# Grouped-query attention on one core: the schedule table laid over 16 pairs of heads in place of 8, with 11 of 64 score tiles on VectorE

## The chip, the cores and the metric

The kernel runs on one NeuronCore of a Trainium2 chip, in one launch. The metric is device time in microseconds (us). TensorE (PE in the profile) multiplies matrices, and its weight loads have a row of their own (PEld); VectorE is DVE, ScalarE is ACT, GpSimd is POOL, and SyncE (SP) issues DMAs, as GpSimd does too. PSUM is the memory that TensorE writes to, SBUF the one that the other data lies in.

## The reference

```python
batch, seq, n_heads, n_kv_heads, dim = 8, 512, 32, 8, 64
scores = np.einsum('bhqd,bhkd->bhqk', Q, K_expanded) * scale      # scale = 1/8
weights = np.exp(scores - np.max(scores, axis=-1, keepdims=True))
weights = weights / (np.sum(weights, axis=-1, keepdims=True) + 1e-10)
output = np.einsum('bhqk,bhkd->bhqd', weights, V_expanded)
```

Four query heads share one K head and one V head (`np.repeat` on the head axis). Q, K and V are fp32 in HBM, the output is fp32.

## The kernel before

**Units and pairs.** The work is cut into 32 units: one batch and two neighbouring K heads (`gp`), with their eight query heads. A unit has 4 pairs of query heads, so there are 128 pairs. A pair has 4 score tiles, one for each 128 keys (`kc`): two matmuls put the scores of both heads, 128 keys by 512 queries each, into one PSUM tile of 128x1024 (`scores`, L235). There are 512 such tiles.

**The exponential on ScalarE.** For most tiles one ACTIVATE reads the PSUM tile and writes `pt` (`exp_act`, L253). These tiles lie in `s_ps`, of which there are two buffers: the scores of tile k can't begin before ScalarE has read tile k-2.

**The exponential on VectorE and GpSimd.** For the others (`DVE_KCS`) it is made of integer operations, in a chain of five instructions: `u`, scale and round from PSUM to 16-bit integers (`exp_bits`, L264, VectorE); `f`, the low ten bits (`exp_low`, L269, VectorE); `g`, a linear step (`slope`, L274, GpSimd); `w`, the product g*f (`bend`, L281, GpSimd); and the sum u+w, which is written as the bits of `pt` (`exp_join`, L285, VectorE). 5 of the 32 tiles of a period go this way.

**The second matmul.** For each pair 32 matmuls multiply `pt` with V; V carries a column of ones, so that each result has its row sum beside it (`pv`, L295). VectorE takes the reciprocal of the sums (`inverse`, L314) and multiplies (`norm`, L324). When a unit is complete, one DMA of 1 MB stores it; in the very last unit each pair has a store of its own, 256 KB (`norm`, `store`).

**PSUM regions.** Beside the two `s_ps` buffers there are two regions of the same size, `d_ps` (letter a in the table) and `pv` (letter b). Each holds one thing at a time: a VectorE score tile, the sums of a pair, or the turned Q of a half unit (`transposes`, L400, eight matmuls with the identity, then a VectorE copy, L194). The next user waits until VectorE has read the one before.

**Order.** Everything is issued in an order written out by hand, the table `STEPS`, which is walked once for each period of 8 pairs (two units, half a batch); `FINISH` replaces it in the last of the 16 periods (L530). A token is a letter and a number: `S` score tile for ScalarE, `A` its ACTIVATE, `V7.1-3` matmuls of pair 7, chunks 1 and 2 of 8 (4 matmuls each; the chunks 6 and 7 hold the keys whose exponential VectorE makes, where it makes one), `R` reciprocal, `N` normalisation, `T` and `C` turning Q and its copy, `K` and `H` a check of V and its reduction, `D` a score tile for VectorE, and `U F G W P` its chain (`g`, `w` in lower case: on VectorE instead). `Q` issues loads, `B` collects checks of the sums, `E` the end. `@1` means that the token belongs to the period before, `@-1` to the one after. An engine works in the order in which its own tokens stand; between engines semaphores decide. In what follows, step k is the stretch from `S`k to `S`k+1.

**Loads.** Q, K and V are loaded by GpSimd DMAs that convert to bf16 (L128 to L148); K is turned by DMA transposes on SP, followed by two copies between partitions (`dma_k`, L176). In a period, `Q0` loads K or V of the next batch, in turn, and `Q1` half a batch of Q two periods ahead (`loads`, L388). In the first period the start-up has its own loads, transposes on TensorE (`EARLY`, L213) and idle matmuls (`spin`, L487) in place of the missing tokens of a period before. In that period the tiles of the first two pairs all go to ScalarE (`on_dve`, L220).

Of the kernel before, what the change touches and what calls it, by code (L numbers as in the profile page):

```python
# [34 lines left out]
VV_HI = 1.0e30  # L35


DVE_KCS = ((3,), (3,), (), (3,), (), (3,), (3,), ())
STEPS = (
# [9 lines left out]
).split()  # L49
FINISH = (  # L50
# [31 lines left out]
def fast_path(ctx, tc, Q, K, V, out, flag):  # L82
# [32 lines left out]
    off = const_pool.tile([128, PPAIR * 2 * SC], U32, name="off")  # L115
# [94 lines left out]
    def early_k(gp, g, lo=0):  # L210
        return lambda bank: first_k(gp, g, bank, lo)

    EARLY = {0: [early_k(0, 0, SC // 2)], 1: [early_q(0, 1)], 2: [early_k(0, 1)],  # L213
             4: [early_q(1, 0)], 5: [early_k(1, 0)], 6: [early_k(1, 1)]}

    every = [(p, kc) for p in range(PPAIR) for kc in range(SC)]
    ON_DVE = [(p, kc) for p, kc in every if kc in DVE_KCS[p]]
    ON_ACT = [(p, kc) for p, kc in every if kc not in DVE_KCS[p]]

    def on_dve(n, k):  # L220
        return n * PPAIR + ON_DVE[k][0] >= NPAIR
# [49 lines left out]
            out=st["f"], in_=st["u"], scalar=1023, op=ALU.bitwise_and  # L271
        )

    def slope(engine, f, g):  # L274
        engine.tensor_scalar(  # L275
            out=g, in0=f, scalar1=-EXP_F1,
            scalar2=EXP_K * 2.0 ** (24 * (engine is nc.gpsimd)),
            op0=ALU.add, op1=ALU.mult,
        )

# [27 lines left out]
                    stop=(n == SC - 1 and qc == SC - 1),  # L308
                )

    RCOLS = PPAIR * 2 * SC
    right = const_pool.tile([128, RCOLS + 1], BF16, name="right")

    def inverse(p):  # L314
        n, k = divmod(p, PPAIR)
        if n not in invs:
            invs[n] = inv_pool.tile([128, PPAIR, 2, SC], FP32, name="inv")
        s = 0 if p % UPAIR < NPAIR else D
        nc.vector.reciprocal(out=invs[n][:, k], in_=sums[p][:, :, :, s:s + 1])  # L319
        done["inv", n] = done.get(("inv", n), 0) + 1  # L320
        if n == NPER - 1 and done["inv", n] == PPAIR:
            last_check()

    def norm(p):  # L324
        u, b, gp, g, i = place(p)
        if u not in osb:
            osb[u] = osb_pool.tile([128, SC, 2 * HPG, D], FP32, name="o_sb")
        h = 2 * (p % UPAIR)
        o = 1 - g
        nc.vector.tensor_tensor(  # L330
            out=osb[u][:, :, h:h + 2, :].rearrange("p qc m d -> p m qc d"),
            in0=sums.pop(p)[:, :, :, o:o + D],
            in1=invs[p // PPAIR][:, p % PPAIR, :, :, None].to_broadcast((128, 2, SC, D)),
            op=ALU.mult,
        )
# [6 lines left out]
    def bulk_check(n):  # L342
        nc.vector.scalar_tensor_tensor(  # L343
            out=off, in0=invs[n].rearrange("p s m qc -> p (s m qc)").bitcast(U32),
            scalar=INV_BITS, in1=off, op0=ALU.bitwise_xor, op1=ALU.bitwise_or,
        )
# [71 lines left out]
    def step(tok, n):  # L418
        what, k = tok[0], int(tok[1:].split(".")[0].rstrip("ab"))
        q, kc = ON_DVE[k] if what in "DUFGWPgwsa" else (0, 0)  # L420
        if what == "S":
# [4 lines left out]
                    copy()  # L426
            if k == 9 and n == 0:
                dma_k(0, TURNED)
            if k == 2 and n % 2 == 1 and n // 2 + 1 < B:
                dma_k(n // 2 + 1)  # L430
        elif what == "A":
            q, kc = ON_ACT[k]
            p = n * PPAIR + q
# [8 lines left out]
        elif what in "VRN":  # L442
            p = n * PPAIR + k
            if what == "V":
                lo, hi = tok[3:].rstrip("abs").split("-")
                pv(p, int(lo), int(hi), tok)
            else:
                (inverse if what == "R" else norm)(p)
        elif what in "TKCH":
            j = n * PPAIR // NPAIR + k  # L450
            if j < 2:
                pass
            elif what == "T":
                transposes(j, region(tok))
            elif what == "K":
                check_values(j)
            else:
                read(j if what == "C" else (j, "v"))
        elif what == "Q":
            loads(n, k)  # L460
        elif what == "B":
            if n < NPER - 1:
                bulk_check(n)
        elif what == "E":
            (early_check, verdict)[k]()
        elif what in "sa":
            (fill if what == "s" else exp_act)(n * PPAIR + q, kc)
        elif on_dve(n, k):
            p = n * PPAIR + q
            if what == "D":  # L470
                exp_fill(p, kc, region(tok))
                return
            st = chain.get((p, kc))
            if what == "U":
                exp_bits(st)
            elif what == "F":
                exp_low(st)
            elif what in "Gg":
                slope(nc.gpsimd if what == "G" else nc.vector, st["f"], st["g"])
# [48 lines left out]
    nc.vector.tensor_copy(out=kn[0][:, mid:hi, 0:2, :], in_=k_start[1][:, mid:hi, :, :])  # L528

    for period in range(-2, NPER):  # L530
        for entry in STEPS if period < NPER - 1 else FINISH:
            tok, _, late = entry.partition("@")
            n = period - int(late or 0)
            if 0 <= n < NPER:
                step(tok, n)
            elif period == 0 and n < 0 and tok[0] == "V":
                lo, hi = tok[3:].rstrip("abs").split("-")
                spin(int(hi) - int(lo), S // 4)
# [117 lines left out]
```

## Time and profile before

| | us |
|---|---|
| median of 3 runs (411.78 to 411.85) | 411.80 |
| the profiled execution | 411.91 |
| its span, first to last instruction | 410.1 |
| ScalarE busy in the span | 399.9 |
| TensorE busy (weight loads beside it: 242.2) | 377.7 |
| VectorE busy | 334.1 |
| GpSimd busy | 276.6 |

The 1.81 us between the span and the execution's time lie around the span. "Busy" is the union of the records of an engine; a matmul's record lasts longer than the time until the next can begin. In the rows of groups the columns are: line, engine, operation, written tile, read tiles, shape, count | busy us, mean ns of one | idle us before it and who ended it. In timelines: start us, duration us, engine, line, operation. In windows: from and to, length, then busy us and count for PE, PEld, DVE, ACT and POOL, granted TensorE clock, DMA share, GB/s.

### The profile page before, as it was taken

How to read it: one execution, taken by the hardware profiler on the slowest of the kernel's cores; microseconds unless marked ns; L12 is line 12 of the kernel's file. 1: busy time of each engine (PE TensorE's matmuls, PEld its weight loads, DVE VectorE, ACT ScalarE, POOL GpSimd, SP SyncE). 2: the span in 40 equal slices, each digit the busy share in tenths (PEclk: the TensorE clock that was granted, in tenths of full speed). 3: DMA queues.
4: the chain of work that ended last, by engine and by line, in shares of the span. 5: the costliest groups of instructions: out<-in, count | busy, mean ns of one | idle time of the engine just before them, and what ended most of it. 6: DMA issues, size and time to landing. Idle time of an engine off the chain costs nothing.

```text
span 410.1 us, 13319 instructions
## 1 busy us (share of the span) xinstructions
PE 377.7 (92%) x5824; PEld 242.2 (59%) x5824; DVE 334.1 (81%) x618; ACT 399.9 (98%) x437; POOL 276.6 (67%) x208
## 2 busy tenths in 40 slices
PE   7989999899998989989899998999989899998994
PEld 3556656565665656656565665656656566565663
DVE  2587888978889788797978889788798878889895
ACT  5999999999999999999999999999999999999994
POOL 9157776677666667676676776667776677765760
PEclk9999999999999999999999999999999999999999
DMA  9999876798659797479865888849788697762206
GB/s 149 196 195 153 192 154 178 181 172 175 159 149 187 119 247 160 140 180 250 158 143 117 193 221 155 206 106 172 195 156 202 160 172 167 157 173 104 78 29 209
DMA packets 65406, 67.74 MB, mean 165 GB/s; under 512 B 35264, under 2 KB 39872, under 8 KB 65344
## 3 DMA queue, kind: packets, MB, share of 16 engines
q0 software_dynamic: 28128, 24.91, 41.5%
q1 hardware_dynamic: 37216, 41.95, 33.7%
q8 instruction: 46, 0.75, 0.7%
q14 instruction: 16, 0.13, 0.1%
HBM read 50.33 MB, written 33.55 MB: 205 GB/s over the span
## 4 chain that ended last, share of the span: by engine, by line
ACT 77%; PE 20%; issue 1%; DVE 1%; ACTq 0%
ACT pt L254 77%; PE s_ps L240 9%; PE pv L303 6%; PE d_ps L303 4%; PE pv L492 1%; PE d_ps L191 0%; DVE qt L194 0%; ACTq L254 0%; DVE o_sb L330 0%; PE s_ps L191 0%; PE d_ps L170 0%; PE d_ps L202 0%; DVE warm L517 0%; DVE kt_first L172 0%; DVE off L343 0%
## 5 line engine op out<-in xcount | busy, mean ns | idle before, releaser
L254 ACT ACTIVATE pt<-s_ps 128x1024 f16<-128x1024 f32 x434 | 398.0, 1292 | 2.2 <-PE s_ps L240 2.2
L303 PEld LDWEIGHTS <-pt 128*128 128x128 f16 x4096 | 142.3, 98 | 64.9 <-issue 55.9
L240 PE MATMUL s_ps<-qt,kt 64*128 64x512 bf16 x810 | 158.7, 383 | 23.2 <-ACT pt L254 19.7
L283 POOL TENSOR_TENSOR w<-g,f 128x1024 bf16<-128x1024 bf16 x77 | 163.9, 2128 | 6.4
L275 POOL TENSOR_SCALAR g<-f 128x1024 bf16<-128x1024 int16 x77 | 80.8, 1049 | 113.2 <-DVE f L270 113.2
L303 PE MATMUL pv<-v,pt 128*128 128x65 bf16 x2560 | 113.9, 195 | 0.4 <-ACT pt L254 0.4
L240 PEld LDWEIGHTS <-kt 64*128 64x128 bf16 x960 | 57.5, 93 | 65.0 <-issue 34.5
L265 DVE TENSOR_SCALAR u<-d_ps 128x1024 int16<-128x1024 f32 x47 | 57.4, 1221 | 19.9 <-PE d_ps L240 19.9
L303 PE MATMUL d_ps<-v,pt 128*128 128x65 bf16 x1536 | 66.3, 194 | 0.0
L330 DVE TENSOR_TENSOR o_sb<-pv,inv 128x512 f32<-128x512 f32 x80 | 55.3, 691 | 2.7
L287 DVE TENSOR_TENSOR pt<-u,w 128x1024 uint16<-128x1024 int16 x78 | 53.4, 685 | 2.2 <-POOL w L283 0.8
L191 PEld LDWEIGHTS <-q_nat 128*128 128x128 bf16 x512 | 29.1, 98 | 15.1 <-issue 11.1
L265 DVE TENSOR_SCALAR u<-pv 128x1024 int16<-128x1024 f32 x31 | 37.7, 1216 | 0.0
L194 DVE COPY qt<-d_ps 128x1024 bf16<-128x1024 bf16 (+1 forms) x48 | 32.6, 680 | 3.7 <-PE d_ps L191 3.7
L330 DVE TENSOR_TENSOR o_sb<-d_ps,inv 128x512 f32<-128x512 f32 x48 | 33.2, 691 | 1.6
L270 DVE TENSOR_SCALAR f<-u 128x1024 int16<-128x1024 int16 x78 | 33.5, 429 | 0.1
L191 PE MATMUL d_ps<-ident,q_nat 128*128 128x128 bf16 x380 | 29.5, 220 | 0.1
L319 DVE RECIPROCAL inv<-pv 128x8 f32<-128x8 f32 x80 | 16.5, 206 | 10.5 <-PE pv L303 7.5
L319 DVE RECIPROCAL inv<-d_ps 128x8 f32<-128x8 f32 x48 | 9.9, 207 | 14.8 <-PE d_ps L303 14.3
L240 PE MATMUL d_ps<-qt,kt 64*128 64x512 bf16 x88 | 17.1, 375 | 0.0
L203 DVE TENSOR_REDUCE okv<-d_ps 128x1 f32<-128x128 f32 x31 | 8.9, 288 | 9.4 <-PE d_ps L202 9.3
L148 POOL DMA_DIRECT2D q_nat<-in_Q_dram x18 | 14.7, 815 | 0.0
(48 smaller groups left out, 112.8 us busy)
## 6 DMA issues: line engine op xcount, KB each, us to landing
out_dram<-o_sb SPq DMA_DIRECT2D x31, 1024.0 KB, 5.1
q_nat<-in_Q_dram POOLq DMA_DIRECT2D x15, 1024.0 KB, 8.9
k_nat<-in_K_dram POOLq DMA_DIRECT2D x7, 512.0 KB, 5.2
kt<-kt SPq DMA_DIRECT2D x14, 256.0 KB, 4.6
v<-in_V_dram POOLq DMA_DIRECT2D x7, 512.0 KB, 7.4
out_dram<-o_sb SPq DMA_DIRECT2D x4, 256.0 KB, 3.1
q_nat<-in_Q_dram POOLq DMA_DIRECT2D x1, 512.0 KB, 8.0
v<-in_V_dram POOLq DMA_DIRECT2D x4, 128.0 KB, 8.6
```

Of the source, the lines that this page charges most:

```text
L191: nc.tensor.transpose(ps[:, i, sc, :], qn[u // 2][:, sc, h:h + 2, :], ident)
L194: return lambda: nc.vector.tensor_copy(out=qt[u][:, g, lo:hi, :], in_=ps[:, lo:hi, :, :].rearrange("p i sc c -> p i (sc c)"))
L240: nc.tensor.matmul(ps[:, m, :], keys[64 * m:64 * m + 64, g if early else g ^ m, kc * 128:(kc + 1) * 128], qt[u][64 * m:64 * m + 64, g, i, ...
L254: nc.scalar.activation(out=pt_of(p)[:, kc, :, :], in_=filled.pop((p, kc)), func=EXP, scale=scale)
L265: nc.vector.tensor_scalar(out=st["u"], in0=st["ps"], scalar1=A_U, scalar2=B_U, op0=ALU.mult, op1=ALU.add)
L270: nc.vector.tensor_single_scalar(out=st["f"], in_=st["u"], scalar=1023, op=ALU.bitwise_and)
L275: engine.tensor_scalar(out=g, in0=f, scalar1=-EXP_F1, scalar2=EXP_K * 2.0 ** (24 * (engine is nc.gpsimd)), op0=ALU.add, op1=ALU.mult,)
L283: engine.tensor_tensor(out=w, in0=g, in1=f, op=ALU.mult)
L287: nc.vector.tensor_tensor(out=pt_of(p)[:, kc, :, :].bitcast(U16), in0=st["u"], in1=st["w"], op=ALU.add)
L303: nc.tensor.matmul(sums[p][:, m, qc, :], pt_of(p)[:, kc, m, qc * 128:(qc + 1) * 128], vt[b % 2][:, kc, gp, g * (D + 1):(g + 1) * (D + 1)], ...
L319: nc.vector.reciprocal(out=invs[n][:, k], in_=sums[p][:, :, :, s:s + 1])
L330: nc.vector.tensor_tensor(out=osb[u][:, :, h:h + 2, :].rearrange("p qc m d -> p m qc d"), in0=sums.pop(p)[:, :, :, o:o + D], in1=invs[p // ...
```

## The change

The table is laid over 16 pairs (four units, a whole batch) in place of 8, so there are 8 periods in place of 16. Of the 64 tiles of a period 11 go to VectorE, where two periods before had 10. In two of the eleven chains the product `w` runs on VectorE (`w2`, `w8`); nine stay on GpSimd. A period issues one K load, two Q loads (1 MB each) and one V load, at `Q0` to `Q3`. The first period has a table of its own, `FIRST`, and the last a new `FINISH`. In the first period the early transposes `EARLY` 4, 5 and 6 move one step ahead, and the idle matmuls have 64 columns in place of 128. The DMA transposes of K are issued at `S31` of each period in place of `S2` of each second one. The checks of the sums stay in groups of 8 pairs (`CPAIR`); `inv` has six buffers in place of three.

```diff
-DVE_KCS = ((3,), (3,), (), (3,), (), (3,), (3,), ())
+DVE_KCS = ((3,), (3,), (), (3,), (3,), (), (3,), (3,), (), (3,), (3,), (), (3,), (3,), (3,), ())
 STEPS = (
...
+    "A0 P10@1 V15.5-6@1 V13.0-1b@1 S1 F0 V15.6-7@1 Q0 A1 V15.7-8@1 V13.1-2@1 G0 V13.2-3@1 "
+    "R15@1 V13.3-4@1 N15@1 S2 A2 V13.4-8@1 W0 S3 R13@1 D2a A3 N13@1 S4 U2 V14.0-1b@1 A4 "
...
+    "A38 V9.2-4 S39 V9.4-5 P7 A39 V9.5-8 S40 F8 T7a R9 A40 B0@2 N9 G8 K7 S41 C7 A41 V10.0-3b "
+    "Q2 w8 S42 V10.3-4 A42 V10.4-6 H7 V10.6-7 P8 S43 A43 V10.7-8 F9 S44 R10 G9 D10a N10 A44 "
+    "U10 S45 V11.0-1b W9 V11.1-2 A45 V11.2-8 S46 R11 A46 N11 S47 V12.0-4a A47 P9 T0b@-1 F10 "
+    "S48 A48 C0@-1 V12.4-6 G10 V12.6-8 S49 R12 D1b@-1 A49 N12 S50 W10 U1@-1 T1a@-1 A50 K1@-1 "
+    "S51 A51 C1@-1 D0b@-1 S52 H1@-1 Q3 U0@-1 V15.0-1a A52 V15.1-4 S0@-1 V15.4-5 "
+).split()
+FIRST = (
...
+    "V14.2-4@1 P0 A5 V14.4-8@1 F1 S6 R14@1 A6 T2a G1 N14@1 S7 C2 D2a U2 Q0 A7 V0.0-3b W1 S8 "
+    "D3a A8 V0.3-4 U3 V0.4-5 S9 V0.5-6 A9 V0.6-8 S10 R0 P1 V2.0-2a A10 V2.2-4 F2 S11 N0 "
...
 FINISH = (
...
+    "V11.7-8 P9 V13.2-3 A49 S51 P10 V13.3-8 A50 R11 S52 R13 N13 A51 V15.0-2s E0 V15.2-4 N11 "
+    "V15.4-6 A52 V15.6-8 B0@2 V14.0-2a R15 V14.2-6 N15 V14.6-8 R14 N14 E1 "
...
     EARLY = {0: [early_k(0, 0, SC // 2)], 1: [early_q(0, 1)], 2: [early_k(0, 1)],
-             4: [early_q(1, 0)], 5: [early_k(1, 0)], 6: [early_k(1, 1)]}
+             3: [early_q(1, 0)], 4: [early_k(1, 0)], 5: [early_k(1, 1)]}
...
     def loads(n, k):
-        b, odd = divmod(n, 2)
-        if k == 0 and b + 1 < B:
-            (load_v if odd else load_k)(b + 1)
-        if k == 1 and n + 2 < NPER:
-            load_q(n + 2)
+        if n + 1 < B:
+            (lambda: load_k(n + 1), lambda: load_q(2 * n + 2),
+             lambda: load_v(n + 1), lambda: load_q(2 * n + 3))[k]()
...
-            if k == 2 and n % 2 == 1 and n // 2 + 1 < B:
-                dma_k(n // 2 + 1)
+            if k == 31 and n + 1 < B:
+                dma_k(n + 1)
...
     for period in range(-2, NPER):
-        for entry in STEPS if period < NPER - 1 else FINISH:
+        for entry in FIRST if period == 0 else STEPS if period < NPER - 1 else FINISH:
...
-                spin(int(hi) - int(lo), S // 4)
+                spin(int(hi) - int(lo), S // 8)
```

For comparison, the table of before has around its steps 6 to 10, and `FINISH` at its end:

```python
"V6.2-4@1 S6 P0 V6.4-6@1 A6 V6.6-7@1 F1 V6.7-8@1 S7 R6@1 G1 T2a N6@1 A7 S8 C2 V0.0-1b W1 "
"V0.1-2 A8 V0.2-3 S9 D2a V0.3-4 A9 U2 V0.4-5 S10 V0.5-7 A10 V0.7-8 B0@2 S11 P1 V1.0-2a "
...
"R6 V7.2-4 N6 V7.4-6 B0@2 A26 V7.6-8 R7 N7 E1 "
```

More of the change, by code (lines that the diff above doesn't have):

```diff
@@ L94, in fast_path @@
     TURNED = 2
+    CPAIR = PPAIR // 2
     scale = 1.0 / math.sqrt(D)
@@ L106, in fast_path @@
     osb_pool = ctx.enter_context(tc.tile_pool(name="osb", bufs=3))
-    inv_pool = ctx.enter_context(tc.tile_pool(name="inv", bufs=3))
+    inv_pool = ctx.enter_context(tc.tile_pool(name="inv", bufs=6))
     PS = bass.MemoryType.PSUM
@@ L114, in fast_path @@
     ident = const_pool.tile([128, 128], BF16, name="ident")
-    off = const_pool.tile([128, PPAIR * 2 * SC], U32, name="off")
+    off = const_pool.tile([128, CPAIR * 2 * SC], U32, name="off")
     okv = const_pool.tile([128, NU + 1], FP32, name="okv")
@@ L218, in fast_path @@
     ON_ACT = [(p, kc) for p, kc in every if kc not in DVE_KCS[p]]
+    BENT_BY_DVE = {int(t[1:].partition("@")[0]) for t in STEPS if t[0] == "w"}
     def on_dve(n, k):
@@ L272, in exp_low, with slope @@
         )
-    def slope(engine, f, g):
+    def slope(engine, f, g, small):
         engine.tensor_scalar(
-            out=g, in0=f, scalar1=-EXP_F1,
-            scalar2=EXP_K * 2.0 ** (24 * (engine is nc.gpsimd)),
+            out=g, in0=f, scalar1=-EXP_F1, scalar2=EXP_K * 2.0 ** (24 * small),
             op0=ALU.add, op1=ALU.mult,
@@ L309, in pv @@
                 )
-    RCOLS = PPAIR * 2 * SC
+    RCOLS = CPAIR * 2 * SC
     right = const_pool.tile([128, RCOLS + 1], BF16, name="right")
     def inverse(p):
-        n, k = divmod(p, PPAIR)
+        n, k = divmod(p, CPAIR)
         if n not in invs:
-            invs[n] = inv_pool.tile([128, PPAIR, 2, SC], FP32, name="inv")
+            invs[n] = inv_pool.tile([128, CPAIR, 2, SC], FP32, name="inv")
         s = 0 if p % UPAIR < NPAIR else D
@@ L320, in inverse @@
         done["inv", n] = done.get(("inv", n), 0) + 1
-        if n == NPER - 1 and done["inv", n] == PPAIR:
+        if n == 2 * NPER - 1 and done["inv", n] == CPAIR:
             last_check()
@@ L332, in norm @@
             in0=sums.pop(p)[:, :, :, o:o + D],
-            in1=invs[p // PPAIR][:, p % PPAIR, :, :, None].to_broadcast((128, 2, SC, D)),
+            in1=invs[p // CPAIR][:, p % CPAIR, :, :, None].to_broadcast((128, 2, SC, D)),
             op=ALU.mult,
@@ L342, in bulk_check @@
     def bulk_check(n):
+        done["checks"] = done.get("checks", 0) + 1
         nc.vector.scalar_tensor_tensor(
@@ L355, in last_check @@
     def last_check():
-        bulk_check(NPER - 1)
+        bulk_check(2 * NPER - 1)
+        assert done["checks"] == 2 * NPER
         nc.vector.tensor_single_scalar(
@@ L380, in probe @@
         nc.gpsimd.memset(f, 512)
-        slope(nc.gpsimd, f, g)
+        slope(nc.gpsimd, f, g, True)
         bend(nc.gpsimd, f, g, w)
@@ L444, in step @@
             if what == "V":
-                lo, hi = tok[3:].rstrip("abs").split("-")
+                lo, hi = tok.split(".")[1].rstrip("abs").split("-")
                 pv(p, int(lo), int(hi), tok)
@@ L461, in step @@
         elif what == "B":
-            if n < NPER - 1:
-                bulk_check(n)
+            if 2 * n + k < 2 * NPER - 1:
+                bulk_check(2 * n + k)
         elif what == "E":
@@ L478, in step @@
             elif what in "Gg":
-                slope(nc.gpsimd if what == "G" else nc.vector, st["f"], st["g"])
+                slope(nc.gpsimd if what == "G" else nc.vector, st["f"], st["g"],
+                      what == "G" and k not in BENT_BY_DVE)
             elif what in "Ww":
@@ L536, in fast_path @@
             elif period == 0 and n < 0 and tok[0] == "V":
[L537 to L538 removed]
+                lo, hi = tok.split(".")[1].rstrip("abs").split("-")
+                spin(int(hi) - int(lo), S // 8)
 def general_path(tc, Q, K, V, out):
```

58 rows, old and new, of tables (FINISH, FIRST, STEPS) are left out of this document.

## The prediction

> **What bounds the kernel now.** I read the chain of work that ended last first, then the groups, then the windows, one to a period.
>
> ```profile
> ACT 77%; PE 20%; issue 1%; DVE 1%; ACTq 0%
> L254 ACT ACTIVATE pt<-s_ps 128x1024 f16<-128x1024 f32 x434 | 398.0, 1292 | 2.2 <-PE s_ps L240 2.2
> ```
> ```profile
> 211.75:236.49 24.74, 23.13 (x364) 14.89 (x363) 20.80 (x39) 24.74 (x28) 17.12 (x12) 1.00 0.73 165
> 236.49:261.24 24.75, 23.12 (x364) 14.91 (x364) 20.81 (x39) 24.75 (x28) 17.75 (x12) 1.00 0.83 177
> ```
> ```profile
> L254 ACT ACTIVATE pt<-s_ps x434: 1018/1313/1349, 6.6 to 403.4; 128x1024 f16<-128x1024 f32 x145
> ```
>
> ScalarE is busy for all of each period (24.75 of 24.75 us, 27 tiles): one tile in 24.75/27 = 0.917 us. Its 434 tiles need 398 of the span's 410.1 us, and it was idle for 2.2 us, before its first tile. So the time is start + tiles x 0.917 + end, as long as every score tile is there when ScalarE wants it. How much later may one be? An ACTIVATE takes 1018 ns where it is quickest and 1313 in the median. I read the difference, 0.30 us, as time for which its record stands behind the one before: a score tile up to about 0.30 us late costs nothing, and what is beyond that ScalarE loses.
>
> **What goes: eight tiles.** Before, 16 x 27 tiles + 2 of the first pairs = 434. After, 8 x 53 + 2 = 426, as the built order of ScalarE shows too. The gain is 8 x 0.917 = **7.33 us**. The rest asks what the others make of a period of 53 x 0.917 = 48.6 us in place of two of 24.75 (49.5).
>
> **Engine sums for a period.** TensorE: the same matmuls (a tile moves from S to D); 2 x 23.13 = 46.3 of 48.6. VectorE:
>
> ```profile
> 248.75 0.21 DVE L319 RECIPROCAL inv<-pv 128x8 f32<-128x8 f32 x1
> 248.99 0.69 DVE L330 TENSOR_TENSOR o_sb<-pv,inv 128x512 f32<-128x512 f32 x1
> 249.60 1.22 DVE L265 TENSOR_SCALAR u<-d_ps 128x1024 int16<-128x1024 f32 x1
> 250.78 0.69 DVE L194 COPY qt<-pv 128x1024 bf16<-128x1024 bf16 x1
> 251.39 0.68 DVE L287 TENSOR_TENSOR pt<-u,w 128x1024 uint16<-128x1024 int16 x1
> 251.99 0.42 DVE L270 TENSOR_SCALAR f<-u 128x1024 int16<-128x1024 int16 x1
> 252.33 1.22 DVE L265 TENSOR_SCALAR u<-pv 128x1024 int16<-128x1024 f32 x1
> ```
> ```profile
> L283 DVE TENSOR_TENSOR w<-g,f 128x1024 bf16<-128x1024 bf16 x1 | 0.7, 682 | 0.0
> ```
>
> From start to start: R 0.24, N 0.61, U 1.18, C 0.61, P 0.60, F 0.34. A product on VectorE has a record as long as P's, so 0.60. One more chain is 2.12, two products are 1.20: 2 x 20.81 + 3.32 = 44.9 of 48.6, 92% against 84%. It still fits, but no longer with much room.
>
> The chain itself goes round: F, then GpSimd's g and w, then P, then the next F.
>
> ```profile
> 246.78 0.42 DVE L270 TENSOR_SCALAR f<-u 128x1024 int16<-128x1024 int16 x1
> ```
> ```profile
> 247.30 1.03 POOL L275 TENSOR_SCALAR g<-f 128x1024 bf16<-128x1024 int16 x1 [1.06 <-DVE f L270]
> 248.41 2.13 POOL L283 TENSOR_TENSOR w<-g,f 128x1024 bf16<-128x1024 bf16 x1
> ```
>
> F to the end of w is 3.76 us, P adds 0.60: 4.36 a round, and with the product on VectorE 0.52 + 1.03 + 0.05 + 0.60 + 0.60 = 2.80. Nine and two: 44.8 of 48.6, where ten took 43.6 of 49.5. That fits too, so on sums ScalarE stays the bound. What is lost must come from single places where a score tile is late.
>
> **Late tiles in every period.** TensorE works in order, so a step longer than 0.917 makes the next S late. The longest block of the trace:
>
> ```profile
> 398.30 0.39 PE L240 MATMUL s_ps<-qt,kt 64*128 64x512 bf16 x2
> 398.63 0.78 PE L303 MATMUL d_ps<-v,pt 128*128 128x65 bf16 x20
> 399.33 0.39 PE L240 MATMUL s_ps<-qt,kt 64*128 64x512 bf16 x2
> ```
> ```profile
> 403.20 1.04 PEld L303 LDWEIGHTS <-pt 128*128 128x128 f16 x32 [0.23 <-DVE right L351]
> ```
>
> 20 matmuls of a pair make a step of 1.03 us; 32 weight loads take 1.04, so 0.03 each. Step 45 holds all 32 matmuls of pair 11: 1.03 + 12 x 0.03 = 1.39, and S46 comes 0.47 late, 0.17 beyond the allowance. Step 47 (16 of pair 12, then T0) makes S48 about as late, but behind a loss that S46 has already cost. I followed the other steps with the intervals above, VectorE's waits included: S51 comes out at most 0.28 late (T1 waits for N12), S0 0.22, the others less. The term is 0.17 in each of the 7 periods that use this order: **+1.2 us**, from 0 (allowance 0.5) to 2.5 (S51 over it as well).
>
> **A hole in the first period.** In `FIRST`, step 7 puts `D2a` straight behind T2 in the same region: T2, its copy C2, D2, U2, D3 follow one another. In the other periods D2 stands at step 3. What such a row costs, the start of before shows:
>
> ```profile
> 14.25 0.39 PE L240 MATMUL s_ps<-qt,kt_first 64*128 64x512 bf16 x2
> 14.57 0.62 PE L191 MATMUL d_ps<-ident,q_nat 128*128 128x128 bf16 x8
> 15.23 0.69 DVE L194 COPY qt<-d_ps 128x1024 bf16<-128x1024 bf16 x1 [0.78 <-PE d_ps L191]
> ...
> 16.27 0.39 PE L240 MATMUL d_ps<-qt,kt_first 64*128 64x512 bf16 x2
> 16.59 0.42 PE L303 MATMUL pv<-v,pt 128*128 128x65 bf16 x8
> 16.70 1.23 DVE L265 TENSOR_SCALAR u<-d_ps 128x1024 int16<-128x1024 f32 x1 [0.78 <-PE d_ps L240]
> 16.97 0.39 PE L240 MATMUL s_ps<-qt,kt_first 64*128 64x512 bf16 x2
> ```
>
> From S6 at 0: T2 at 0.32, its copy ends 15.92 - 14.57 = 1.35 later (1.67), D2 at 1.72, U2 ends 0.43 + 1.23 later (3.38), D3 at 3.43. Behind D3 stand two chunks, and S9 follows 16.97 - 16.27 = 0.70 after D3: 4.13. It is due at 3 x 0.917 = 2.75; 1.38 late less 0.30 is **+1.1 us**, once (S8 is late by less on the way). Below: 0, if something ahead runs early; above: 1.4, without the allowance.
>
> **The end.** Before, ScalarE ended at 397.88 + 6.79 = 404.67, and 5.43 us followed.
>
> ```profile
> 397.88 6.79 ACT pt L254 x8
> ```
> ```profile
> 400.00:402.00 2.00, 2.00 (x45) 1.39 (x41) 1.97 (x5) 2.00 (x4) 0.00 (x0) 1.00 0.98 359
> 402.00:404.00 2.00, 1.95 (x44) 1.47 (x43) 1.36 (x6) 2.00 (x3) 0.00 (x0) 1.00 0.98 316
> ```
>
> After, behind the last A there stand not 8 matmuls but 40, since pair 14 comes wholly behind it: 32 x 0.03 = 0.96 later until the last R. Unit 30's store of 1 MB also moves: it waited for N3 at step 21 of 27, and now for N11 in the last step, about 0.5 us behind ScalarE's end. With the small stores about 1.8 MB then go out; at 340 GB/s, as in the windows, that is 5.4 us, about 1 us longer than the calculation hides. I take **+1.4 us**, from 0.9 (stores hidden) to 2.4 (nothing of them hidden).
>
> Costed at nothing: the loads. Q has 23 steps (21 us) from issue to first use, V 19 (17 us), against these landings (V is as large as K); if one took nearly twice as long it would still be there.
>
> ```profile
> q_nat<-in_Q_dram POOLq DMA_DIRECT2D x15, 1024.0 KB, 8.9
> k_nat<-in_K_dram POOLq DMA_DIRECT2D x7, 512.0 KB, 5.2
> ```
>
> SP issues the turning of K behind the store of the unit before, and TensorE first reads it at step 49. The early transposes and idle matmuls lie under the first ScalarE tiles.
>
> **Sum.** 410.1 - 7.33 + 1.2 + 1.1 + 1.4 = 406.5 of span; with the 1.81 around it 408.3; the profiled execution was 0.11 above the median, so **408.1 us** against 411.80.
>
> **The rivals.**
>
> *Nothing is lost inside.* If the allowance is wider than I read it and the first period's hole closes, 7.33 less 0.9 of end remains: 405.4. For it: two periods of before run without any loss at 93% of TensorE. Against: no step there was as long as 1.39.
>
> *VectorE becomes the bound (slower).* From step 40 to the next period's step 0 the order has for VectorE 3 F, 4 R, 4 N, 3 C, one product, 3 P, 3 U: 1.02 + 0.96 + 2.44 + 1.83 + 0.60 + 1.80 + 3.54 = 12.2 us, and three short checks, in 14 steps of 12.8 us. D0, D1, T0 and T1 of the next period wait for it, and behind them S. Twenty-four instructions that are each 0.03 us slower, or one wait of 0.7 that I overlooked, cost 0.6 in each of 7 periods, 4.2 us: from there the change loses. With 1.0 us it is 408.1 + 6.6 = 414.7. Against: these intervals repeat to 0.01 us from period to period.
>
> *VectorE and GpSimd hold each other up.*
>
> ```profile
> L270 DVE TENSOR_SCALAR f<-u x78: 415/420/1026, 18.0 to 397.0; 128x1024 int16<-128x1024 int16 x78
> ```
>
> One F took 1026 ns: it began while GpSimd was still in a product. A meeting of this kind costs 0.61 us, one in each period's full stretch 7 x 0.6 = 4.2 us: 412.2, no change. Against: in the table F of a chain stands directly behind P of the one before, P waits for GpSimd's w, and the next g waits for F, so GpSimd is between products when P and F run. [...]
>
> *An early load comes late.* In `FIRST` the K load of the next batch stands ahead of any product on GpSimd, directly behind the probe.
>
> ```profile
> 10.07 0.20 POOL L283 TENSOR_TENSOR probe_w<-probe_g,probe_f 128x2 bf16<-128x2 bf16 x1
> ...
> 21.66 0.62 POOL L131 DMA_DIRECT2D k_nat<-in_K_dram  x1
> ```
>
> So it starts some 11 us earlier than before, while the start-up's loads are still in flight. If the turned K of batch 0 came 2 us late for its first use (step 26), 408.1 + 2 = 410. Against: that use stands three steps later than before, since pair 8 has no tile on VectorE now.
>
> **Chances.** Forecast (406.8 to 409.8) 0.58; nothing lost 0.18; VectorE bound 0.13; holding up 0.06; late load 0.05. The range, 405.4 to 411.0, holds the first two and the last, 0.81; its ends are the bounds of the terms. A measurement here can tell 0.2%, 0.8 us, from no change: faster 0.58 + 0.18 + 0.05 = 0.81, same 0.06, slower 0.13.
>
> **What would show it.** 426 ACTIVATEs; ScalarE idle about 1.1 us between 14 and 18 us and about 0.17 before one tile in each 48.7 us; TensorE's waits there on VectorE's copy and u; 6.8 us behind the last ACTIVATE, with the DMA engines full. It is wrong if windows of 48.6 us hold more than 0.5 us of ScalarE's idle time, if the loss sits in steps 49 to 0 before S (VectorE's stretch), or if F or g have records well above 0.42 and 1.04.

## The result, and the profile after

The changed kernel takes **409.87 us** (median of 6 runs, 409.54 to 410.78) against 411.79 (6 runs, 411.68 to 413.12): a ratio of 0.9951, 95% interval 0.9935 to 0.9966. It is faster by 1.9 us, where 3.7 were forecast. The profiled execution took 410.04 us, with a span of 408.3.

The timeline of ScalarE (start, duration, engine, line, operation, count, then the idle time ahead and who ended it; records that touch are run together) is the whole balance. First before, then after:

```profile
6.60 398.07 ACT L254 ACTIVATE pt<-s_ps 128x1024 f16<-128x1024 f32 x434 [2.16 <-PE s_ps L240]
```
```profile
6.75 9.36 ACT L292 ACTIVATE pt<-s_ps 128x1024 f16<-128x1024 f32 x10 [1.96 <-PE s_ps L278]
16.36 1.02 ACT L292 ACTIVATE pt<-s_ps 128x1024 f16<-128x1024 f32 x1 [0.24 <-PE s_ps L278]
17.95 382.09 ACT L292 ACTIVATE pt<-s_ps 128x1024 f16<-128x1024 f32 x415 [0.56 <-PE s_ps L278]
```

10 + 1 + 415 = 426 tiles, as forecast. They run from 6.75 to 17.95 + 382.09 = 400.04, 393.29 us, where 434 took 398.07: 4.78 us less, not the 7.33 that eight tiles are worth. Then 408.3 - 400.04 = 8.26 us follow; it was 5.43. So of 7.33 us there were given back:

| given back | us | forecast |
|---|---|---|
| first tile later (6.75 for 6.60) | 0.15 | 0 |
| holes in the first period, ahead of the 11th and 12th tile | 1.0 | 1.1 |
| one late tile in each of 7 periods | 1.6 | 1.2 |
| end, behind the last ACTIVATE | 2.8 | 1.4 |
| sum | 5.5 | 3.7 |

7.33 - 5.5 = 1.8, as the spans say (410.1 and 408.3). An idle time in the rows is not yet a loss: records of ScalarE overlap when it is well fed (before, records of 1292 ns in the mean came every 0.917 us). I take as loss what the end of a record lies more than 0.917 us behind the end of the one before: 0.35 and 0.67 us in the first period, 0.22 in each later one.

The window of one period of 48.80 us, the chain and the groups of the changed kernel:

```profile
84.30:133.10 48.80, 46.01 (x720) 29.22 (x720) 44.15 (x81) 48.68 (x54) 33.85 (x25) 1.00 0.83 173
```
```profile
PE 53%; ACT 34%; DVE 10%; issue 1%; ACTq 0%
L292 ACT ACTIVATE pt<-s_ps 128x1024 f16<-128x1024 f32 x426 | 391.7, 1117 | 3.6 <-PE s_ps L278 2.8
```

ScalarE is still the bound: 48.68 us busy in 48.80, with TensorE at 46.0 (forecast 46.3) and VectorE at 44.1 (44.9). The chain has turned from 77% ScalarE to 53% TensorE all the same. It follows what came last, and a score tile that arrives just in time counts there as much as one that is late; the mean record of an ACTIVATE has fallen from 1292 to 1117 ns for the same reason, since fewer of them stand behind the one before. Neither view says that TensorE limits the time as a whole. The windows do not say so; what the experiments find is single blocks on TensorE, above all in step 45, that make one tile late.

### The profile page after: what moved, and what is told of

Read it like the earlier page. It is cut to its first block, busy times and chain, and to the rows that moved or that the text cites. A ratio compares the mean times of both kernels' runs of the same rounds, so it can differ in the third digit from the quotient of the medians.

```text
span 408.3 us, 13344 instructions
## 1 busy us (share of the span) xinstructions
PE 376.0 (92%) x5820; PEld 237.3 (58%) x5820; DVE 354.6 (87%) x660; ACT 393.6 (96%) x429; POOL 264.3 (65%) x206
## 4 chain that ended last, share of the span: by engine, by line
PE 53%; ACT 34%; DVE 10%; issue 1%; ACTq 0%
ACT pt L292 34%; PE s_ps L278 20%; PE pv L340 16%; PE d_ps L340 8%; DVE u L303 5%; PE d_ps L227 3%; DVE o_sb L367 3%; PE d_ps L278 2%; DVE qt L230 1%; PE pv L530 1%; PE pv L227 1%; DVE inv L356 1%; DVE okv L239 0%; PE d_ps L238 0%; PE s_ps L340 0%
## 5 line engine op out<-in xcount | busy, mean ns | idle before, releaser
L292 ACT ACTIVATE pt<-s_ps 128x1024 f16<-128x1024 f32 x426 | 391.7, 1117 | 3.6 <-PE s_ps L278 2.8
L313 POOL TENSOR_SCALAR g<-f 128x1024 bf16<-128x1024 int16 x84 | 87.5, 1041 | 118.9 <-DVE f L308 118.9
L320 POOL TENSOR_TENSOR w<-g,f 128x1024 bf16<-128x1024 bf16 x68 | 144.4, 2124 | 5.7
L340 PE MATMUL pv<-v,pt 128*128 128x65 bf16 x2752 | 121.3, 195 | 2.0 <-DVE o_sb L367 1.9
L303 DVE TENSOR_SCALAR u<-d_ps 128x1024 int16<-128x1024 f32 x64 | 78.0, 1219 | 13.5 <-PE d_ps L278 13.5
L324 DVE TENSOR_TENSOR pt<-u,w 128x1024 uint16<-128x1024 int16 x86 | 59.0, 686 | 5.9 <-POOL w L320 4.6
L340 PE MATMUL d_ps<-v,pt 128*128 128x65 bf16 x1312 | 56.0, 194 | 0.7
L303 DVE TENSOR_SCALAR u<-pv 128x1024 int16<-128x1024 f32 x22 | 26.7, 1215 | 0.0
L278 PE MATMUL d_ps<-qt,kt 64*128 64x512 bf16 x120 | 23.2, 379 | 1.3 <-DVE u L303 1.2
L230 DVE COPY qt<-pv 128x1024 bf16<-128x1024 bf16 x16 | 11.0, 688 | 1.4 <-PE pv L238 1.3
```

The lines of the kernel that those rows point to most:

```text
L230: return lambda: nc.vector.tensor_copy(out=qt[u][:, g, lo:hi, :], in_=ps[:, lo:hi, :, :].rearrange("p i sc c -> p i (sc c)"))
L278: nc.tensor.matmul(ps[:, m, :], keys[64 * m:64 * m + 64, g if early else g ^ m, kc * 128:(kc + 1) * 128], qt[u][64 * m:64 * m + 64, g, i, ...
L292: nc.scalar.activation(out=pt_of(p)[:, kc, :, :], in_=filled.pop((p, kc)), func=EXP, scale=scale)
L303: nc.vector.tensor_scalar(out=st["u"], in0=st["ps"], scalar1=A_U, scalar2=B_U, op0=ALU.mult, op1=ALU.add)
L313: engine.tensor_scalar(out=g, in0=f, scalar1=-EXP_F1, scalar2=EXP_K * 2.0 ** (24 * small), op0=ALU.add, op1=ALU.mult,)
L320: engine.tensor_tensor(out=w, in0=g, in1=f, op=ALU.mult)
```

## The experiments

The theory is the sum of the prediction with the sizes of the table above: a hole in `FIRST`, step 45, and a late store at the end. The rivals are that the losses sit elsewhere (in VectorE's full stretch, from step 40 to the next step 0; in the early loads; in the shorter idle matmuls). Each kernel is the changed one with the edit shown; best joins two of them.

| label | median, us (lowest to highest) | ratio to before, 95% interval |
|---|---|---|
| first_d2 | 408.95 (408.21 to 410.55) | 0.9921, 0.9901 to 0.9942 |
| old_spin | 409.92 (409.42 to 410.10) | 0.9944, 0.9927 to 0.9961 |
| skip_v11 | 409.26 (409.08 to 409.36) | 0.9929, 0.9912 to 0.9946 |
| skip_v11_v12 | 408.08 (407.24 to 409.41) | 0.9894, 0.9874 to 0.9914 |
| f9_thrice | 414.37 (414.04 to 414.62) | 1.0055, 1.0034 to 1.0077 |
| w8_pool | 426.31 (424.77 to 426.71) | 1.0333, 1.0307 to 1.0360 |
| end_n11 | 408.95 (408.68 to 409.31) | 0.9922, 0.9904 to 0.9939 |
| end_swap | 407.95 (407.52 to 408.90) | 0.9900, 0.9879 to 0.9920 |
| best | 407.06 (406.74 to 407.12) | 0.9868, 0.9840 to 0.9897 |

The kernels were measured in three rounds, and the median of before was 411.91, 412.02 and 411.81 in them (411.79 beside the changed kernel). So differences of 0.2 us between medians are not read.

### The hole in the first period: first_d2

```diff
 FIRST
-P0 A5 V14.4-8@1 F1 S6 ... S7 C2 D2a U2 Q0 A7
+P0 A5 D2b U2 F1 S6 ... S7 C2 Q0 A7
```

> FIRST alone is changed: D2 goes into region b at step 5 (in place of four idle matmuls) and its u ahead of C2, so T2, C2 and D3 no longer wait for D2 and U2. Theory (the first period loses 1.02 us of ScalarE time, 0.35 + 0.67 at its 11th and 12th tiles, because T2, C2, D2, U2, D3 stand in one chain on one region): both losses go, 409.9 - 1.0 = 408.9, and nothing else in the trace moves but by that shift. Rival (the first tiles are late because the start-up's loads, among them the earlier K load, hold something up): the two losses stay and the time is 409.9.

(`V14.4-8@1` has no period before it here, and stands for idle matmuls.)

The timeline of the changed kernel shows the row of steps on one region that the prediction followed, each waiting for the one before:

```profile
13.73 0.62 PE L227 MATMUL d_ps<-ident,q_nat 128*128 128x128 bf16 x8
...
14.39 0.69 DVE L230 COPY qt<-d_ps 128x1024 bf16<-128x1024 bf16 x1 [1.20 <-PE d_ps L227]
15.14 0.39 PE L278 MATMUL d_ps<-qt,kt_first 64*128 64x512 bf16 x2 [0.41 <-DVE qt L230]
15.57 1.22 DVE L303 TENSOR_SCALAR u<-d_ps 128x1024 int16<-128x1024 f32 x1 [0.48 <-PE d_ps L278]
15.93 0.39 PE L278 MATMUL s_ps<-qt,kt_first 64*128 64x512 bf16 x2
...
16.84 0.39 PE L278 MATMUL d_ps<-qt,kt_first 64*128 64x512 bf16 x2 [0.52 <-DVE u L303]
17.52 0.39 PE L278 MATMUL s_ps<-qt,kt_first 64*128 64x512 bf16 x2
```

T2 (13.73), its copy (14.39), D2 (15.14), U2 (15.57), D3 (16.84), and S8 and S9 behind them at 15.93 and 17.52. S9 begins 17.52 - 13.73 = 3.79 behind T2; the prediction had 4.13 - 0.32 = 3.81. With D2 in the other region and two steps earlier both losses are gone: the ScalarE records of first_d2 run through there, and the median falls by 0.92 us, of 1.02 that the two losses are worth. In best, which has this edit too, the tiles run through at the same place. So this hole is shown.

The profiled execution of first_d2 (410.55) is its slowest, and its timeline gives a reason: a pair of score matmuls takes 0.61 us in the first tiles, not 0.39. Those tiles lose about 0.9 us by it, so that the last ACTIVATE of this profile ends at 9.21 + 390.73 = 399.94, hardly ahead of the changed kernel's 400.04. The gain is read from the median and from best.

```profile
6.10 0.61 PE L278 MATMUL s_ps<-qt,kt_first 64*128 64x512 bf16 x2 [0.40 <-DVE kt_first L208]
9.67 0.61 PE L278 MATMUL s_ps<-qt,kt_first 64*128 64x512 bf16 x2
11.47 0.39 PE L278 MATMUL s_ps<-qt,kt_first 64*128 64x512 bf16 x2
```

The edit does not cause this: the first of these rows stands ahead of it, and the profile of skip_v11_v12, which does not have the edit, shows the same. It comes back below.

### The idle matmuls at the start: old_spin

```diff
-                spin(int(hi) - int(lo), S // 8)
+                spin(int(hi) - int(lo), S // 4)
```

> The idle matmuls of the first period have 128 columns again, as before the change; nothing else. In the profiles so far TensorE's matmuls ran at half speed until 5 to 7 us in some executions and until 10.5 us in others (score pairs of 0.61 us instead of 0.39), with some 0.8 us of ScalarE lost in the latter. Theory (the shorter idle matmuls make the late clock likelier): the spread of the executions shrinks and the median is 0.2 to 0.5 us lower, 409.4 to 409.7. Rival (when the clock rises is chance, and the length of these matmuls has no part in it): 409.9 with the same spread, or slightly more where the longer matmuls hold S up.

No difference in the median: 409.92 against 409.87, and the two holes stay (0.42 and 0.67). So the theory, 0.2 to 0.5 us less, did not come true, and the shorter idle matmuls cost nothing that can be measured. The six executions lie within 0.7 us where those of the changed kernel span 1.2; that is too few to say whether slow score pairs at the start (0.61 us in place of 0.39) have become rarer. The earlier transposes were not tested by themselves.

### Step 45: skip_v11 and skip_v11_v12

```diff
 STEPS and FIRST, skip_v11
-V11.1-2 A45 V11.2-8 S46
+V11.1-2 A45 V11.2-4 V11.6-8 S46
 and skip_v11_v12 besides
-V12.0-4a A47
+V12.0-2a A47
```

> Leaves out 8 of the 32 second matmuls of pair 11 in the first seven periods (its chunks 4 and 5), so step 45 has 24 matmuls instead of 32. Prediction's theory: S46 comes 0.25 late instead of 0.49 and costs nothing, but S48, whose lateness (0.46) stood hidden behind S46's, now shows and costs about 0.17 to 0.2 a period: time 409.4 to 409.8. Rival A (S46's block is the only loss of a period): 7 x 0.22 = 1.56 us less, 408.3. Rival B (S46 is late because V11 waits for N10 on VectorE): S46's loss stays at 0.22, 409.9.

> Leaves out the same 8 matmuls of pair 11 and 8 of pair 12 (its chunks 2 and 3) in the first seven periods, so step 47 has 8 fewer too. Prediction's theory: no tile of a period is late beyond the allowance, 7 x 0.22 = 1.56 us less than the changed kernel, 408.3, and no ACTIVATE of periods 1 to 6 shows a gap. Rival (VectorE's stretch from step 40 to step 0 is full and sets the period): the loss reappears at S49 to S52 or S0, and the time stays above 409.

Step 45 in the timeline of the changed kernel (TensorE; the last row is S46 and S47 together):

```profile
99.00 0.39 PE L278 MATMUL s_ps<-qt,kt 64*128 64x512 bf16 x2 [0.31 <-ACT pt L292]
99.32 1.16 PE L340 MATMUL pv<-v,pt 128*128 128x65 bf16 x32
100.41 0.81 PE L278 MATMUL s_ps<-qt,kt 64*128 64x512 bf16 x4
```

From S45 to S46 it is 100.41 - 99.00 = 1.41 us (forecast 1.39), 0.49 more than a tile lasts, and ScalarE loses 0.22 of it. The allowance is thus 0.49 - 0.22 = 0.27, where I had read 0.30 off the records. ScalarE's 23 tiles across this place in the changed kernel, in skip_v11 and in skip_v11_v12:

```profile
91.40 21.51 ACT L292 ACTIVATE pt<-s_ps 128x1024 f16<-128x1024 f32 x23
```
```profile
91.05 21.45 ACT L292 ACTIVATE pt<-s_ps 128x1024 f16<-128x1024 f32 x23
```
```profile
91.13 21.28 ACT L292 ACTIVATE pt<-s_ps 128x1024 f16<-128x1024 f32 x23
```

With the 8 matmuls of pair 11 left out, S46 comes in time, yet only 0.06 of the 0.23 us comes back: S48 now loses 0.12 (0.17 to 0.2 were expected) and S51 0.04. Only when step 47 loses 8 matmuls too is the period clean. Neither rival of skip_v11 holds: S46's block is not the only loss, and S46 does not stay late. That is what the prediction said of S48 (about as late, but behind a loss that S46 has already cost): the two are not added, and mending one brings the other out. The medians agree in order, less well in size: -0.6 and -1.8 us for 7 x 0.06 = 0.4 and 7 x 0.23 = 1.6 (409.4 to 409.8 and 408.3 were expected, 409.26 and 408.08 measured). Both kernels do less work, so they only locate the loss. No order was tried that does all the work without it.

### How full VectorE's stretch is: f9_thrice

```diff
 STEPS and FIRST
-V10.7-8 F9 S44
+V10.7-8 F9 F9 F9 S44
```

> VectorE does f of chain 9 three times instead of once in the first seven periods: 2 x 0.34 = 0.68 us more in the stretch from step 40 to step 0 that the prediction named as VectorE's full one. The prediction's claim (the stretch is full, so 0.7 us more there cost about 0.6 a period): 7 x 0.6 = 4.2 us on top, about 414, with gaps at S45 to S52. Rival (VectorE waits often enough in the stretch to take it up, its share there is not a bound): 409.9 to 410.5.

VectorE in the changed kernel and in f9_thrice:

```profile
97.68 0.42 DVE L308 TENSOR_SCALAR f<-u 128x1024 int16<-128x1024 int16 x1
...
98.25 0.69 DVE L367 TENSOR_TENSOR o_sb<-pv,inv 128x512 f32<-128x512 f32 x1
```
```profile
98.19 1.34 DVE L308 TENSOR_SCALAR f<-u 128x1024 int16<-128x1024 int16 x3
99.68 0.69 DVE L367 TENSOR_TENSOR o_sb<-pv,inv 128x512 f32<-128x512 f32 x1
```

From F9's start to N10's start it is 1.49 us in place of 0.57: a repeated F, which writes the same tile, takes (1.34 - 0.42) / 2 = 0.46, so VectorE was given 0.92 us and not the 0.68 that I meant. The next rows are TensorE's S45 and pair 11 in f9_thrice, and ScalarE's S46:

```profile
99.50 0.39 PE L278 MATMUL s_ps<-qt,kt 64*128 64x512 bf16 x2 [0.31 <-ACT pt L292]
100.42 1.16 PE L340 MATMUL pv<-v,pt 128*128 128x65 bf16 x32 [0.53 <-DVE o_sb L367]
```
```profile
102.00 1.02 ACT L292 ACTIVATE pt<-s_ps 128x1024 f16<-128x1024 f32 x1 [0.71 <-ACT pt L292]
```

Pair 11 now waits for N10 (99.68 + 0.69 = 100.37) and begins 0.92 behind S45; in the changed kernel it was 0.32, with N10 over at 98.25 + 0.69 = 98.94, 0.38 before. So of 0.92 us 0.32 was room and 0.60 is late, and ScalarE's loss at S46 grows by just that, from 0.22 to 0.82. The median rises by 414.37 - 409.87 = 4.5 us, 0.64 a period (S51 gives another 0.06). That the number expected came out is luck: more was added, and there was more room. The rival "VectorE becomes the bound" has its mechanism shown, with 0.32 us between the changed kernel and its edge.

### A product on GpSimd instead: w8_pool

```diff
 STEPS and FIRST (in FINISH w8 -> W8 alone)
-V10.0-3b Q2 w8 S42
+V10.0-3b W8 Q2 S42
```

> Undoes one of the two products on VectorE: w8 runs on GpSimd again, at the same place in the order, ahead of the V load. Theory (VectorE works in order, so P8 behind it has to wait for 2.1 us of GpSimd instead of 0.6 us of its own, and F9, R10 and N10 come later, and with them V11): VectorE is idle for about 1 us before P8, S46 is later by 0.3 to 0.6, and the time is 2 to 4 us longer, 412 to 414. Rival (VectorE's work is what is short in this stretch, so 0.6 us less of it helps): at or under 409.9.

Slower, as expected, but by 16.4 us where 2 to 4 were expected. VectorE, then GpSimd:

```profile
99.39 0.69 DVE L324 TENSOR_TENSOR pt<-u,w 128x1024 uint16<-128x1024 int16 x1 [1.74 <-POOL w L320]
100.00 0.75 DVE L308 TENSOR_SCALAR f<-u 128x1024 int16<-128x1024 int16 x1
```
```profile
97.23 2.12 POOL L320 TENSOR_TENSOR w<-g,f 128x1024 bf16<-128x1024 bf16 x1
99.30 1.22 POOL L173 DMA_DIRECT2D v<-in_V_dram  x1
```

P8 waits 1.74 us for the product, and F9, behind it in VectorE's order, takes 0.75 in place of 0.42 beside GpSimd's issue of the V load. N10 is later, and pair 11's matmuls wait for it. So far it is f9_thrice again. The rest is in ScalarE's timeline, period by period:

```profile
53.10 48.76 ACT L292 ACTIVATE pt<-s_ps 128x1024 f16<-128x1024 f32 x53 [1.35 <-issue]
104.22 48.80 ACT L292 ACTIVATE pt<-s_ps 128x1024 f16<-128x1024 f32 x53 [2.35 <-issue]
```

The first time ScalarE idles 1.35 us, the second and each of the later five 2.34 to 2.36. TensorE's timeline at the same two places, and the windows of the second (the column behind POOL is the granted TensorE clock):

```profile
51.53 1.16 PE L340 MATMUL pv<-v,pt 128*128 128x65 bf16 x32 [1.17 <-DVE o_sb L367]
...
101.64 1.94 PE L340 MATMUL pv<-v,pt 128*128 128x65 bf16 x32 [1.17 <-DVE o_sb L367]
```
```profile
100.00:102.00 2.00, 0.75 (x9) 0.46 (x9) 1.97 (x5) 1.86 (x3) 1.59 (x3) 0.87 0.19 17
102.00:104.00 2.00, 2.00 (x33) 1.55 (x30) 1.06 (x3) 0.00 (x0) 2.00 (x1) 0.50 1.74 171
104.00:106.00 2.00, 2.00 (x30) 1.20 (x26) 1.69 (x4) 1.78 (x2) 0.51 (x2) 0.78 1.03 168
```

The same wait of 1.17 us, the same 32 matmuls: 1.16 us the first time, 1.94 the second, at a granted clock of 0.50. So about 1.0 of the 2.35 us a period is not the wait but the clock that fell at its end. The expectation had the wait, but with a loss of 0.3 to 0.6 us a period, and nothing of the clock. An idle time of 1.35 us is a loss of 1.45 (the record behind it lasts 1.02, not 0.917), 1.23 more than the 0.22 of the changed kernel. As sums, the wait alone makes 7 x 1.23 = 8.6 us and the clock 6 x 1.0 = 6.0; the other 1.8 us are small losses behind S46 in each period, 0.5 in the last period (ScalarE idles 0.37 us ahead of its tile at 409.33) and a longer end.

### The end: end_n11 and end_swap

```diff
 FINISH, end_n11
-A50 R11 S52 R13 N13 A51 V15.0-2s E0 V15.2-4 N11 V15.4-6
+A50 R11 N11 S52 R13 N13 A51 V15.0-2s E0 V15.2-4 V15.4-6
 FINISH, end_swap: pairs 11 and 12 exchanged in V, R and N, from step 44 on
-P7 V12.0-1a ... R12 N12 ... A50 R11 S52 ... N11 V15.4-6
+P7 V11.0-1a ... R11 N11 ... A50 R12 S52 ... N12 V15.4-6
```

> FINISH alone is changed: N11 stands directly behind R11 instead of behind R13, N13 and the check of V, so the 1 MB store of unit 30 starts about 1.2 us earlier. Theory (the end is longer than forecast because the DMA engines are still moving the late 1 MB store when the last small one is issued): the 8.3 us behind the last ACTIVATE become about 7.0, time 408.7. Rival (the end is set by the 40 matmuls behind the last ACTIVATE and the last pair's reciprocal, check and product): the same 8.3 us, 409.9.

> FINISH alone is changed: pairs 11 and 12 change places in it (V, R and N), so the 1 MB store of unit 30 waits for an N that stands at step 48 instead of 52, and pair 12's 256 KB store goes out late in its place. Same work, same order of engines. Theory (the end is set by the late 1 MB store): about 4 us of head start for 1 MB leave 1 MB behind the last ACTIVATE, which 340 GB/s move in 3.1 us, ahead of the last product's own 2.8 + 3.6 us; 8.3 us behind the last ACTIVATE become 6.4 to 6.6, time about 408.1. Rival (VectorE's and TensorE's own work at the end sets it): 8.3 stays, 409.9; what is left over 5.4 is theirs in either case.

The windows of the changed kernel from 400 us on (the last two columns are DMA share and GB/s):

```profile
400.00:402.00 2.00, 1.48 (x43) 1.29 (x40) 1.75 (x6) 0.04 (x1) 0.00 (x0) 1.00 0.80 270
402.00:404.00 2.00, 0.19 (x1) 0.08 (x1) 0.92 (x4) 0.00 (x0) 0.00 (x0) 1.00 1.02 376
404.00:406.00 2.00, 0.00 (x0) 0.00 (x0) 0.00 (x0) 0.00 (x0) 0.00 (x0) 1.00 0.89 269
406.00:408.30 2.30, 0.00 (x0) 0.00 (x0) 0.00 (x0) 0.00 (x0) 0.00 (x0) 0.54 0.08 23
```
```profile
399.61 0.68 DVE L367 TENSOR_TENSOR o_sb<-pv,inv 128x512 f32<-128x512 f32 x1
...
402.15 0.68 DVE L367 TENSOR_TENSOR o_sb<-d_ps,inv 128x512 f32<-128x512 f32 x1
```

N11 ends at 400.29, and only then can unit 30's 1 MB go. From 400 on 2 x (270 + 376 + 269) + 2.3 x 23 = 1883 KB leave, and the last product, N14, is over at 402.83: behind it 5.5 us of the span go by with stores alone. The last small store, issued at 402.9, lands 4.3 us later; in before and in end_swap it takes 2.3 us. Before, 3.6 us followed the last normalisation (405.79 + 0.68 = 406.47 to 410.1). The rows are this normalisation, of before, and N11 in end_n11:

```profile
405.79 0.68 DVE L330 TENSOR_TENSOR o_sb<-pv,inv 128x512 f32<-128x512 f32 x1
```
```profile
398.18 0.69 DVE L367 TENSOR_TENSOR o_sb<-pv,inv 128x512 f32<-128x512 f32 x1
```

In end_n11 N11 moves up by 1.4 us, and the span falls from 408.3 to 407.5. ScalarE ends 0.26 us earlier in that profile (399.78), so 7.7 us remain behind it in place of 8.26, where 7.0 were expected: a part of the loss comes back, and less than expected. In end_swap the whole pair moves up, and the windows show the store going out beside the last tiles:

```profile
398.00:400.00 2.00, 1.59 (x41) 1.27 (x37) 1.85 (x7) 2.00 (x3) 0.00 (x0) 1.00 0.63 235
400.00:402.00 2.00, 1.47 (x43) 1.29 (x40) 1.75 (x6) 0.03 (x1) 0.00 (x0) 1.00 0.78 242
402.00:404.00 2.00, 0.19 (x1) 0.08 (x1) 0.91 (x3) 0.00 (x0) 0.00 (x0) 1.00 0.61 191
```

Nothing else moved: ScalarE's last ACTIVATE ends at 400.03, the last normalisation at 402.82, but the span ends at 406.4, 6.4 us behind ScalarE in place of 8.26. The median falls by 1.9 us. The late store is the cause, and it is shown.

### Both repairs: best

```diff
 first_d2 and end_swap together
```

> The two repairs together: D2 in region b at step 5 of FIRST, and pairs 11 and 12 exchanged in FINISH; the order of the periods between is untouched. Theory (the losses are at separate places and add up): 411.8 - 7.3 + 1.6 (S46 in seven periods) + 1.0 (the end) + 0 = 407.0, that is 1.0 below the exchanged end alone. Rival (the first period's repair only moves its loss into the start-up, where some executions have a late clock): no better than the exchanged end alone, 408.0.

407.06 us: 0.92 and 1.92 us taken from 409.87 make 407.03, so the two add. This version beats both kernels, by 1.0 to 1.6% against before. Its ScalarE rows

```profile
6.32 1.02 ACT L292 ACTIVATE pt<-s_ps 128x1024 f16<-128x1024 f32 x1 [1.72 <-PE s_ps L278]
7.66 391.33 ACT L292 ACTIVATE pt<-s_ps 128x1024 f16<-128x1024 f32 x425 [0.32 <-PE s_ps L278]
```

have no hole left between the second tile and the last. What still goes is 0.22 at S46 in 7 periods, and the wait ahead of the second tile.

## Why the prediction was right, and where it was off

**Eight tiles, 7.33 us:** right. 426 ACTIVATEs, and where the score tiles come in time a tile takes 0.917 us as before.

**The hole in the first period, 1.1 us:** right in place, cause and size (1.02, and first_d2 takes 0.92 of it away).

**Step 45, 1.2 us:** right in place and cause; 1.6 in size. The lateness is 0.49 and not 0.47 (32 weight loads in 1.04 us are 0.0325 each, which the sum rounded to 0.03), and the allowance 0.27 and not 0.30: that leaves 0.22 and not 0.17. The claim that S48 hides behind it held, as did S51's (within the allowance as long as S46 loses).

**The end, 1.4 us:** this term was mis-sized, and it makes most of the difference: 2.8. It had two parts. The matmuls behind the last A were right: N14 ends 402.83 - 400.04 = 2.79 us behind ScalarE, where the last normalisation of before ended 406.47 - 404.67 = 1.80 behind, 0.99 more for 0.96. The store was not: I took 0.4 us for it on the view that the calculation hides most of the 1.8 MB, and it cost 5.47 - 3.63 = 1.84: what follows the last normalisation, after and before. The term as a whole lies beyond its upper bound of 2.4. The step that failed is "about 1 us longer than the calculation hides": the store can't start before N11's end, 0.25 us behind ScalarE's last tile; 2.5 us of arithmetic remain to cover it, and the small stores of the last unit go out in the same time, in windows with a DMA share of 0.80 to 1.02. With the store out of the way (end_swap) 6.4 us remain behind ScalarE, which is the 5.43 + 0.96 that the prediction gave for a hidden store.

**The start, 0:** the first tile came 0.15 us later. Up to the first score pair TensorE has the same instructions in both kernels; the shorter idle matmuls come behind it. The first score pair took 0.61 us in the changed kernel's profile and 0.45 in that of before, at the same 6.10 us; the rows are of after and then of before. It varies between executions, as the last section shows.

```profile
6.10 0.61 PE L278 MATMUL s_ps<-qt,kt_first 64*128 64x512 bf16 x2 [0.39 <-DVE kt_first L208]
...
7.10 0.39 PE L278 MATMUL s_ps<-qt,kt_first 64*128 64x512 bf16 x2
```
```profile
6.10 0.45 PE L240 MATMUL s_ps<-qt,kt_first 64*128 64x512 bf16 x2 [0.40 <-DVE kt_first L172]
```

**The loads, nothing:** right, although K's landing doubled; its load is now issued directly behind a 1 MB load of Q.

```profile
k_nat<-in_K_dram POOLq DMA_DIRECT2D x7, 512.0 KB, 10.4
```

ScalarE has no hole where the turned K is first used.

**The rivals.** "Nothing is lost inside" fell: S46 loses in each period, and the allowance is smaller, not wider. "VectorE becomes the bound" did not come to pass, but f9_thrice shows where it begins: the prediction let a wait of 0.7 us cost 0.6, and 0.92 cost 0.60, so there is 0.2 us more room than it took. (Its second price, 6.6 us for a wait of 1.0, leaves still less room: 7 x 0.9 = 6.3 would go with the first.) "VectorE and GpSimd hold each other up" fell by one row of the changed kernel:

```profile
L308 DVE TENSOR_SCALAR f<-u x86: 373/420/426, 18.5 to 393.8; 128x1024 int16<-128x1024 int16 x86
```

The longest of 86 is 426 ns, where one of 78 had taken 1026 before, and no F or P overlaps a g or a product on GpSimd. The rows of before are GpSimd's product and the long F:

```profile
381.37 2.12 POOL L283 TENSOR_TENSOR w<-g,f 128x1024 bf16<-128x1024 bf16 x1
```
```profile
382.75 1.03 DVE L270 TENSOR_SCALAR f<-u 128x1024 int16<-128x1024 int16 x1
```

The F ended 0.29 us behind the product. Two more F of before began during a product, at 379.30 and at 397.04; they ended 0.29 us behind it too, and took 0.48 and 0.49 us. So such a meeting was seen, at 0.06 to 0.61 us each, and the order of the changed kernel keeps clear of it. What holds the F up was not shown. The late load fell with the hole that is not there.

The time, 409.87, lies above the forecast's 408.1 by 1.8: 1.4 of the end, 0.4 of step 45 and 0.15 of the start, less 0.1 of the first period. It is inside the range of 405.4 to 411.0, but just beyond the forecast's own part of it, 406.8 to 409.8. The ends of the range come from the bounds of all the terms together: the end went past its own bound of 2.4, and step 45, at 1.6 of up to 2.5, left room for that. That the sum stayed inside is in part luck.

## What to carry to other kernels

Price a late store by what is left to hide it: the time from the instruction that releases it to the last arithmetic, not the arithmetic of the whole end; here moving one pair forward was worth as much as the whole change (1.9 us). When an engine is fed just in time, look up each place where its supplier's step is longer than its own, and expect the mend of the worst one to bring out the next. A side engine may be 94% full over a stretch (VectorE in the 12.84 us from S40, at 94.43, on: 12.13 busy) and cost nothing, but put two more instructions there to learn how far the edge is before building on it.

## What the hardware showed that was not expected

**The TensorE clock fell in the middle of the kernel after a short wait.** In w8_pool a wait of TensorE of 1.17 us stands ahead of pair 11, and after the second of these waits the clock fell. From the windows, at half speed: 2 x (1 - 0.87) / 0.5 = 0.52, then 2.0, then 2 x (1 - 0.78) / 0.5 = 0.88, together 3.4 us, from 101.48 on. The windows of the third period give the same sum: 0.32 + 2.0 + 1.08 = 3.4.

```profile
151.00:153.00 2.00, 0.60 (x6) 0.31 (x6) 1.97 (x5) 2.00 (x3) 1.68 (x2) 0.92 0.12 11
153.00:155.00 2.00, 2.00 (x34) 1.70 (x33) 1.07 (x2) 0.01 (x1) 1.92 (x2) 0.50 1.62 157
155.00:157.00 2.00, 2.00 (x30) 1.22 (x26) 1.66 (x4) 1.64 (x2) 0.51 (x2) 0.73 1.13 156
```

In the four periods behind these ScalarE idles as long (2.34 to 2.36 us), and the mean granted clock of the run is 0.973, against 0.997 in the changed kernel: 424.6 x (0.997 - 0.973) / 0.5 = 20.4 us at half speed, six times 3.4. After the first wait, also 1.17 us, no fall followed: the windows from 48 to 56 us have 1.00. In f9_thrice the wait there is 0.53 us, and its windows from 96 to 104 us have 1.00 as well. Why the clock fell after six of these waits and not after the first was not shown.

**TensorE came to its full pace at different times at the start.** In the changed kernel four transposes of q begin 0.107 us apart at 4.72 and 0.056 us apart at 7.42. With the same instructions up to there, the first score pair, at 5.9 to 6.1 us, was already quick (0.39 us) in old_spin and best and took 0.45 us in before, 0.61 in the changed kernel and in end_swap, while first_d2 and skip_v11_v12 still had 0.61 us at 9.67. The moment thus differs by 3.5 us or more between executions. It is read from the durations; the granted clock in the windows up to 20 us (before, the changed kernel, first_d2, skip_v11_v12) is 1.00 all along.

**A short instruction was stretched beside a DMA issue.** In w8_pool F9 took 0.75 us and not 0.42 where it began beside GpSimd's issue of the V load (at 49.89 and at 100.00), and it ended 0.22 to 0.23 us behind the end of the issue both times. P8, just ahead and beside the same issue, kept its 0.69. In the changed kernel, where other instructions run beside the issues, none of 86 was above 0.43. It looks as if F waited for the issue to end, but no run moved the one against the other: an observation in one place of one kernel, no rule.
